# A row-sum kernel: its rows in three contiguous blocks of 16, 96 and 16 per partition, with all but the last 16 results stored early

## The chip, the cores and the metric

The kernel runs on one core of one Trainium2 chip. The metric is the device time of one execution in microseconds, the lower the better.

Two clocks appear in the text. The *time* is what a run is judged by. The *span* is what the profile covers: from the first to the last instruction of the program. A load or store has *landed* when the last of its 16 completions, one per DMA engine, has arrived at its semaphore (a counter on which engines wait).

## The reference

```python
batch, seq, dim = 32, 512, 1024
x = randn(batch, seq, dim).astype(float32)
out = sum(maximum(x, 0), axis=-1)     # float32, shape (32, 512)
```

There are 16384 rows of 1024 floats: 64 MiB are read, 64 KiB are written. Each of the 128 partitions handles 128 rows (J = 128), and `res` holds one result per row, so it is a 128 x 128 tile.

## The kernel before

All input and output DMAs are issued by SP (SyncE) on one queue; ACT is ScalarE, DVE is VectorE. Rows are loaded in seven chunks of 16 rows per partition (8 MB each), into three buffers, then in a tail of 8, 4, 2 and 1 rows, and the last row in two halves of 512 columns. For most chunks ACT applies the relu and DVE sums. In the last full chunk and in the tail both engines do whole rows alone, with an accumulating instruction each.

```python
x0 = xr[0 : P * BIG, :].rearrange("(p j) d -> p j d", p=P)     # block of 16 rows per partition
o0 = of[0 : P * BIG].rearrange("(p j) -> p j", p=P)
xv = xr[P * BIG :, :].rearrange("(p j) d -> p j d", p=P)       # block of 112 rows per partition
ov = of[P * BIG :].rearrange("(p j) -> p j", p=P)
# ... cut: chunks, then the tail loads, from xv ...
sp.dma_start(out=o0[:, :], in_=res[:, 0:BIG]).then_inc(s_out0, 16)    # behind the last load
# ... cut: the compute of chunks and tail ...
act.wait_ge(s_in[-2], 16)          # first half of the last row
on_act(buf[:, tb, BIG - 1, 0 : LAST[0]], last[:, LAST[1] : LAST[1] + 1]).then_inc(s_tact, 1)
dve.wait_ge(s_tact, 1)
dve.wait_ge(s_in[-1], 16)          # second half, with ACT's sum as its 513th column
on_dve(last[:, :], res[:, J - 1 : J]).then_inc(s_tdve, 1)
sp.wait_ge(s_tdve, 1)
sp.dma_start(out=ov[:, :], in_=res[:, BIG:J]).then_inc(s_out, 16)     # 112 results per partition
```

The partition pitch of a block is its number of rows times 4 KB: 64 KB in the block of 16, 448 KB in the block of 112. In the output a partition's results of a block lie in one row: 64 B for 16 rows, 448 B for 112.

Of the kernel before, what the change touches and what calls it, by code (L numbers as in the profile page):

```python
# [2 lines left out]

P = 128
D = 1024
BIG = 16
NBIG = 7
NTWO = 6
NB = 3
STEPS = [4, 5, 7]  # L10
MIXED = [3, 4, 5]
TAIL = [8, 4, 2, 1]
LAST = [512, 512]


def bass_relu_sum_kernel(
    nc: bass.Bass,
    x: bass.AP,
    out: bass.AP,
):  # L20






    fp32 = mybir.dt.float32
    ALU = mybir.AluOpType
    AF = mybir.ActivationFunctionType
    X = mybir.AxisListType.X  # L30

    B, S, _ = x.shape
    J = B * S // P
    assert BIG * NBIG + sum(TAIL) + 1 == J and sum(LAST) == D

    xr = x.rearrange("b s d -> (b s) d")
    of = out.rearrange("b s -> (b s)")
    x0 = xr[0 : P * BIG, :].rearrange("(p j) d -> p j d", p=P)
    o0 = of[0 : P * BIG].rearrange("(p j) -> p j", p=P)
    xv = xr[P * BIG :, :].rearrange("(p j) d -> p j d", p=P)  # L40
    ov = of[P * BIG :].rearrange("(p j) -> p j", p=P)

    buf = nc.alloc_sbuf_tensor("buf", [P, NB, BIG, D], fp32)
    last = nc.alloc_sbuf_tensor("last", [P, LAST[1] + 1], fp32)
    res = nc.alloc_sbuf_tensor("res", [P, J], fp32)

    n_in = NBIG + len(TAIL) + 2
    s_in = [nc.alloc_semaphore(f"s_in{i}") for i in range(n_in)]
    s_act = nc.alloc_semaphore("s_act")
    s_dve = nc.alloc_semaphore("s_dve")  # L50
    s_tact = nc.alloc_semaphore("s_tact")
    s_tdve = nc.alloc_semaphore("s_tdve")
    s_out0 = nc.alloc_semaphore("s_out0")
    s_out = nc.alloc_semaphore("s_out")

    sp, act, dve = nc.sync, nc.scalar, nc.vector


    tb = NBIG % NB
    for c in range(NBIG + 1):  # L60
        if c >= NB:
            sp.wait_ge(s_dve, 3 * (c - NB + 1))
        if c < NBIG:
            sp.dma_start(  # L64
                out=buf[:, c % NB, :, :],
                in_=xv[:, (c - 1) * BIG : c * BIG, :] if c else x0[:, :, :],
            ).then_inc(s_in[c], 16)
    r = 0
    tail = []
    for i, n in enumerate(TAIL):  # L70
        sp.dma_start(  # L71
            out=buf[:, tb, r : r + n, :],
            in_=xv[:, (NBIG - 1) * BIG + r : (NBIG - 1) * BIG + r + n, :],
        ).then_inc(s_in[NBIG + i], 16)
        tail.append((r, n, s_in[NBIG + i]))
        r += n
    sp.dma_start(
        out=buf[:, tb, r, 0 : LAST[0]], in_=xv[:, J - BIG - 1, 0 : LAST[0]]
    ).then_inc(s_in[-2], 16)
    sp.dma_start(out=last[:, 0 : LAST[1]], in_=xv[:, J - BIG - 1, LAST[0] : D]).then_inc(  # L80
        s_in[-1], 16
    )
    sp.dma_start(out=o0[:, :], in_=res[:, 0:BIG]).then_inc(s_out0, 16)


    def on_act(t, acc):
        return act.activation(t, t, AF.Relu, accum_out=acc)  # L87

    def on_dve(t, acc):
        return dve.tensor_scalar(  # L90
            out=t, in0=t, scalar1=0.0, scalar2=None, op0=ALU.max, op1=ALU.add, accum_out=acc
        )

    def row(c, i):
        return buf[:, c % NB, i, :], res[:, c * BIG + i : c * BIG + i + 1]

    for c in range(NTWO):
        b, steps = c % NB, STEPS if c < NTWO - 1 else MIXED
        act.wait_ge(s_in[c], 16)
        if steps is MIXED:  # L100
            dve.wait_ge(s_in[c], 16)
            for i in (BIG - 4, BIG - 3):
                on_dve(*row(c, i))
        r = 0
        for i, n in enumerate(steps):
            t = buf[:, b, r : r + n, :]
            act.activation(t, t, AF.Relu).then_inc(s_act, 1)  # L107
            dve.wait_ge(s_act, 3 * c + i + 1)
            dve.tensor_reduce(  # L109
                out=res[:, c * BIG + r : c * BIG + r + n], in_=t, axis=X, op=ALU.add  # L110
            ).then_inc(s_dve, 1)
            r += n
        if steps is MIXED:
            for i in (BIG - 2, BIG - 1):
                on_act(*row(c, i))


    j0 = NBIG * BIG
    for c in range(NTWO, NBIG):
        act.wait_ge(s_in[c], 16)  # L120
        dve.wait_ge(s_in[c], 16)
        for i in range(BIG):
            (on_act if i % 2 else on_dve)(*row(c, i))
    for r, n, s in tail:
        if n > 1:
            act.wait_ge(s, 16)
        dve.wait_ge(s, 16)
        for i in range(r, r + n):
            f = on_act if (i - r) % 2 else on_dve
            f(buf[:, tb, i, :], res[:, j0 + i : j0 + i + 1])  # L130

    act.wait_ge(s_in[-2], 16)
    on_act(buf[:, tb, BIG - 1, 0 : LAST[0]], last[:, LAST[1] : LAST[1] + 1]).then_inc(s_tact, 1)
    dve.wait_ge(s_tact, 1)
    dve.wait_ge(s_in[-1], 16)
    on_dve(last[:, :], res[:, J - 1 : J]).then_inc(s_tdve, 1)


    sp.wait_ge(s_tdve, 1)
    sp.dma_start(out=ov[:, :], in_=res[:, BIG:J]).then_inc(s_out, 16)  # L140
    sp.wait_ge(s_out0, 16)
    sp.wait_ge(s_out, 16)


# [1 line left out]
_INS = ['x']  # L146
_OUTS = [((32, 512), 'float32')]


# [21 lines left out]
```

## Time and profile before

| | before |
|---|---|
| time, median of the first 3 runs | 162.49 us (162.36 to 162.69) |
| span of the profile | 161.04 us |
| DMA queue, share of 16 engines | 97.1% |
| last piece of the last load completes | 158.57 us |
| last DVE piece | 158.72 to 159.41 us |
| final store, issue to last completion | 159.44 to 161.00 us |

First the page's DMA part of the kernel before (queue and kind, then packets, megabytes and the share of the 16 engines' span).

```profile
q1 hardware_dynamic: 2160, 67.18, 97.1%
HBM read 67.11 MB, written 0.07 MB: 417 GB/s over the span
```

The 16 DMA engines are busy nearly the whole span, so the loads set the time. The packet records of the trace show how evenly: a 64 KB row takes 2.418 us (median; 27.1 GB/s per engine), and the chunks after the first land 19.35 us apart. Now the end of the chain that ended last (start in us, duration, what):

```profile
123.74 34.20 DMA buf<-in_x_dram
157.94 0.02 issue
157.96 0.73 ACT buf L87 x2
158.70 0.02 issue
158.72 0.70 DVE last L90 x2
```

And the DMA issues of the stores (size of one, median us from issue to landing), with the timeline's line of the final one (start, duration on the queue):

```profile
out_dram<-res SPq DMA_DIRECT2D x1, 56.0 KB, 1.6
out_dram<-res SPq DMA_DIRECT2D x1, 8.0 KB, 34.0
```

```profile
159.44 0.34 SPq L140 DMA_DIRECT2D out_dram<-res  x1
```

The early 8 KB store stood 34 us in the queue behind loads, and nobody waited for it. The 56 KB store stands alone behind everything: ACT piece, DVE piece, store, end. Only what shortens this serial end, or the loads, shortens the span. Of the store's 1.56 us, 0.34 us is the issue on SP, about 0.5 us passes until the first packet at 160.28, the packets run until 160.62, and completions come until 161.00.

### The profile page before, as it was taken

The numbers are of one execution on the slowest core, as the hardware profiler recorded it, in microseconds if no ns is written. First come the engines' busy times: TensorE is split into PE (matmuls) and PEld (weight loads), VectorE is DVE, ScalarE is ACT, GpSimd is POOL, SyncE is SP. The second block draws the span as 40 slices with busy tenths as digits, with TensorE's granted clock in tenths as the row PEclk, the third lists the DMA queues.
The fourth block names the chain that finished last, engine by engine and source line by source line (L and its number), as shares of the span: only waits on it lengthen the run. The fifth ranks groups of instructions, "written<-read, shape, count | busy, mean of one in ns | idle before, by whom it ended". The sixth has DMA issues, their size and how long they took to land.

```text
span 161.0 us, 144 instructions
## 1 busy us (share of the span) xinstructions
DVE 122.0 (76%) x56; ACT 101.0 (63%) x55; POOL 0.2 (0%) x4
## 2 busy tenths in 40 slices
DVE  0000004998969898898969989699899999598995
ACT  3000039991599907997099951999339980596972
POOL 0000000000000000000000000000000000000000
DMA  7979979979979979979979979979979969999992
GB/s 260 521 309 472 521 309 472 521 309 472 521 309 472 521 309 472 521 309 472 521 309 472 521 309 472 521 309 472 521 309 472 521 260 521 391 391 431 413 403 71
DMA packets 2160, 67.18 MB, mean 417 GB/s; under 512 B 496, under 2 KB 496, under 8 KB 880
## 3 DMA queue, kind: packets, MB, share of 16 engines
q1 hardware_dynamic: 2160, 67.18, 97.1%
HBM read 67.11 MB, written 0.07 MB: 417 GB/s over the span
## 4 chain that ended last, share of the span: by engine, by line
DMA 69%; ACT 18%; DVE 10%; SPq 1%; issue 0%
DMA buf<-in_x_dram 69%; ACT buf L107 17%; DVE res L109 9%; SPq L71 1%; ACT buf L87 0%; DVE last L90 0%; SPq L64 0%
## 5 line engine op out<-in xcount | busy, mean ns | idle before, releaser
L109 DVE TENSOR_REDUCE res<-buf 128x4 f32<-128x4096 f32 (+3 forms) x18 | 100.4, 5604 | 34.5 <-ACT buf L107 34.5
L107 ACT ACTIVATE buf<-buf 128x4096 f32<-128x4096 f32 (+3 forms) x18 | 80.9, 4555 | 47.3 <-DMA buf<-in_x_dram 47.3
L87 ACT ACTIVATE buf<-buf 128x1024 f32<-128x1024 f32 (+1 forms) x18 | 18.4, 1024 | 9.7 <-DMA buf<-in_x_dram 9.7
L90 DVE TENSOR_SCALAR_CACHE_REDUCE buf<-buf 128x1024 f32<-128x1024 f32 x18 | 21.0, 1216 | 2.7 <-DMA buf<-in_x_dram 2.5
L87 ACT ACTIVATION_READ_ACCUMULATOR buf<-buf 128x1 f32 x18 | 3.4, 189 | 0.0
L107 ACT ACT_TABLE_LOAD x1 | 1.3, 1283 | 0.7 <-PEq L156 0.7
L90 DVE DVE_READ_ACCUMULATOR buf<-buf 128x1 f32 x18 | 1.5, 83 | 0.0
L90 DVE TENSOR_SCALAR_CACHE_REDUCE last<-last 128x513 f32<-128x513 f32 x1 | 0.7, 689 | 0.2 <-ACT buf L87 0.2
L156 POOL MEMSET const-bfloat16-1.0<- 128x1 bf16 x1 | 0.1, 102 | 0.0
L156 POOL MEMSET const-uint8-127<- 128x1 uint8 x1 | 0.1, 102 | 0.0
L156 POOL MEMSET const-float32-0.0<- 128x1 f32 x1 | 0.1, 99 | 0.2 <-issue 0.2
L156 POOL MEMSET const-float32-1.0<- 128x1 f32 x1 | 0.1, 99 | 0.0
L90 DVE DVE_READ_ACCUMULATOR last<-last 128x1 f32 x1 | 0.1, 84 | 0.0
## 6 DMA issues: line engine op xcount, KB each, us to landing
buf<-in_x_dram SPq DMA_DIRECT2D x1, 4096.0 KB, 26.7
buf<-in_x_dram SPq DMA_DIRECT2D x1, 2048.0 KB, 31.2
buf<-in_x_dram SPq DMA_DIRECT2D x1, 1024.0 KB, 33.2
buf<-in_x_dram SPq DMA_DIRECT2D x1, 512.0 KB, 34.0
buf<-in_x_dram SPq DMA_DIRECT2D x1, 256.0 KB, 34.2
last<-in_x_dram SPq DMA_DIRECT2D x1, 256.0 KB, 34.3
buf<-in_x_dram SPq DMA_DIRECT2D x7, 36.3
out_dram<-res SPq DMA_DIRECT2D x1, 56.0 KB, 1.6
```

The lines of the kernel that those rows point to most:

```text
L71: sp.dma_start(out=buf[:, tb, r : r + n, :], in_=xv[:, (NBIG - 1) * BIG + r : (NBIG - 1) * BIG + r + n, :],).then_inc(s_in[NBIG + i], 16)
L87: return act.activation(t, t, AF.Relu, accum_out=acc)
L90: return dve.tensor_scalar(out=t, in0=t, scalar1=0.0, scalar2=None, op0=ALU.max, op1=ALU.add, accum_out=acc)
L107: act.activation(t, t, AF.Relu).then_inc(s_act, 1)
L109: dve.tensor_reduce(out=res[:, c * BIG + r : c * BIG + r + n], in_=t, axis=X, op=ALU.add).then_inc(s_dve, 1)
L156: nc = _bacc.Bacc("TRN2", target_bir_lowering=False, num_devices=1)
```

## The change

The intent is to have nearly all results out before the end: the rows are cut into three blocks, the results of the first two are stored as soon as they are there, behind the last load in the queue, and the final store carries 16 results per partition (64 B rows, 8 KB) in place of 112.

```diff
-NBIG = 7
+REGIONS = [16, 96, 16]
+CHUNKS = [(0, 0), (1, 0), (1, 16), (1, 32), (1, 48), (1, 64), (1, 80)]
 ...
-    x0 = ...; o0 = ...; xv = ...; ov = ...            (as above, two blocks)
+    start = [sum(REGIONS[:i]) for i in range(len(REGIONS))]
+    xv = [xr[P * s : P * (s + n), :].rearrange("(p j) d -> p j d", p=P)
+          for s, n in zip(start, REGIONS)]
+    ov = [of[P * s : P * (s + n)].rearrange("(p j) -> p j", p=P) for s, n in zip(start, REGIONS)]
 ...   (chunks load from xv[g][:, j : j + BIG, :], the tail from xv[-1])
-    sp.dma_start(out=o0[:, :], in_=res[:, 0:BIG]).then_inc(s_out0, 16)
+    sp.wait_ge(s_fact, 1)
+    sp.wait_ge(s_fdve, 1)
+    for g in range(len(REGIONS) - 1):
+        sp.dma_start(out=ov[g][:, :], in_=res[:, start[g] : start[g] + REGIONS[g]]).then_inc(s_store, 16)
 ...   (last two rows of chunk 6:)
-            (on_act if i % 2 else on_dve)(*row(c, i))
+            ins = (on_act if i % 2 else on_dve)(*row(c, i))
+            if i >= BIG - 2:
+                ins.then_inc(s_fact if i % 2 else s_fdve, 1)
 ...
-    sp.dma_start(out=ov[:, :], in_=res[:, BIG:J]).then_inc(s_out, 16)
+    sp.dma_start(out=ov[-1][:, :], in_=res[:, start[-1] : J]).then_inc(s_out, 16)
```

Two things change at once: the size of the final store, and where each partition's rows lie (chunks 1 to 6 have a pitch of 384 KB in place of 448, the tail 64 KB in place of 448).

More of the change, by code (lines that the diff above doesn't have):

```diff
@@ L33, in bass_relu_sum_kernel @@
     J = B * S // P
-    assert BIG * NBIG + sum(TAIL) + 1 == J and sum(LAST) == D
+    NBIG = len(CHUNKS)
+    assert BIG * NBIG + sum(TAIL) + 1 == J == sum(REGIONS) and sum(LAST) == D
     xr = x.rearrange("b s d -> (b s) d")
     of = out.rearrange("b s -> (b s)")
-    x0 = xr[0 : P * BIG, :].rearrange("(p j) d -> p j d", p=P)
-    o0 = of[0 : P * BIG].rearrange("(p j) -> p j", p=P)
-    xv = xr[P * BIG :, :].rearrange("(p j) d -> p j d", p=P)
-    ov = of[P * BIG :].rearrange("(p j) -> p j", p=P)
+    start = [sum(REGIONS[:i]) for i in range(len(REGIONS))]
+    xv = [
+        xr[P * s : P * (s + n), :].rearrange("(p j) d -> p j d", p=P)
+        for s, n in zip(start, REGIONS)
+    ]
+    ov = [of[P * s : P * (s + n)].rearrange("(p j) -> p j", p=P) for s, n in zip(start, REGIONS)]
     buf = nc.alloc_sbuf_tensor("buf", [P, NB, BIG, D], fp32)
@@ L50, in bass_relu_sum_kernel @@
     s_dve = nc.alloc_semaphore("s_dve")
+    s_fact = nc.alloc_semaphore("s_fact")
+    s_fdve = nc.alloc_semaphore("s_fdve")
     s_tact = nc.alloc_semaphore("s_tact")
     s_tdve = nc.alloc_semaphore("s_tdve")
-    s_out0 = nc.alloc_semaphore("s_out0")
+    s_store = nc.alloc_semaphore("s_store")
     s_out = nc.alloc_semaphore("s_out")
@@ L63, in bass_relu_sum_kernel @@
         if c < NBIG:
-            sp.dma_start(
-                out=buf[:, c % NB, :, :],
-                in_=xv[:, (c - 1) * BIG : c * BIG, :] if c else x0[:, :, :],
-            ).then_inc(s_in[c], 16)
+            g, j = CHUNKS[c]
+            sp.dma_start(out=buf[:, c % NB, :, :], in_=xv[g][:, j : j + BIG, :]).then_inc(
+                s_in[c], 16
+            )
     r = 0
@@ L70, in bass_relu_sum_kernel @@
     for i, n in enumerate(TAIL):
-        sp.dma_start(
-            out=buf[:, tb, r : r + n, :],
-            in_=xv[:, (NBIG - 1) * BIG + r : (NBIG - 1) * BIG + r + n, :],
-        ).then_inc(s_in[NBIG + i], 16)
+        sp.dma_start(out=buf[:, tb, r : r + n, :], in_=xv[-1][:, r : r + n, :]).then_inc(
+            s_in[NBIG + i], 16
+        )
         tail.append((r, n, s_in[NBIG + i]))
         r += n
-    sp.dma_start(
-        out=buf[:, tb, r, 0 : LAST[0]], in_=xv[:, J - BIG - 1, 0 : LAST[0]]
-    ).then_inc(s_in[-2], 16)
-    sp.dma_start(out=last[:, 0 : LAST[1]], in_=xv[:, J - BIG - 1, LAST[0] : D]).then_inc(
+    sp.dma_start(out=buf[:, tb, r, 0 : LAST[0]], in_=xv[-1][:, BIG - 1, 0 : LAST[0]]).then_inc(
+        s_in[-2], 16
+    )
+    sp.dma_start(out=last[:, 0 : LAST[1]], in_=xv[-1][:, BIG - 1, LAST[0] : D]).then_inc(
         s_in[-1], 16
     )
-    sp.dma_start(out=o0[:, :], in_=res[:, 0:BIG]).then_inc(s_out0, 16)
+    sp.wait_ge(s_fact, 1)
+    sp.wait_ge(s_fdve, 1)
+    for g in range(len(REGIONS) - 1):
+        sp.dma_start(
+            out=ov[g][:, :], in_=res[:, start[g] : start[g] + REGIONS[g]]
+        ).then_inc(s_store, 16)
     def on_act(t, acc):
@@ L139, in bass_relu_sum_kernel @@
     sp.wait_ge(s_tdve, 1)
-    sp.dma_start(out=ov[:, :], in_=res[:, BIG:J]).then_inc(s_out, 16)
-    sp.wait_ge(s_out0, 16)
+    sp.dma_start(out=ov[-1][:, :], in_=res[:, start[-1] : J]).then_inc(s_out, 16)
+    sp.wait_ge(s_store, 16 * (len(REGIONS) - 1))
     sp.wait_ge(s_out, 16)
```

## The prediction

> **What bounds the kernel.** The loads, at the rate of the 16 DMA engines. The page gives the queue 97.1% of 16 engines' span, 417 GB/s on average. In the trace's packet records every 64 KB row of a full chunk takes 2.418 us (27.1 GB/s per engine) once the start is over, both in chunk 0 (neighbouring partitions 64 KB apart) and in chunks 1 to 6 (448 KB apart); chunks land 19.35 us apart. The chain of waits is 69% DMA, but its ACT and DVE parts lie beside running loads.
>
> After the last load comes a short serial end (chain, timeline): the 512-column ACT piece ends at 158.70 us, the last DVE piece runs 158.72 to 159.41, the final store (56 KB, 128 rows of 448 B) is issued at 159.44, its packets run 160.28 to 160.62, its last completion arrives at 161.00, the end of the span: 1.56 us from issue to landing.
>
> **What the change does.**
> - Bytes, chunks, compute and the order of loads stay. Rows move: chunks 1 to 6 get a partition pitch of 384 KB for 448 KB, the tail 64 KB. The Trainium skill, "DMA: Bandwidth & Descriptors", section Latency and other measured facts, shows losses at 2 MiB pitch and above, and a better rate at 512 KiB. This trace agrees as far as it goes: 64 and 448 KB both give 2.418 us. I expect 0 us.
> - The store of the first 16 columns and a new one of 96 (384 B rows, 48 KB) are issued once chunk 6 is done, about 148.1 us in the timeline; both should be issued by 149.2, after all loads. They drain behind the last load. Before, the 64 B store there took 0.06 us per engine and landed at 158.75, 0.18 us after the last load. With the 384 B rows (0.15 us per engine, scaled from the 448 B store's 0.177) they should land at 158.9 to 159.2, over 1 us before the final store's packets. Cost: 0.
> - The final store shrinks to 64 B rows. An engine's packets take 0.177 us for 8 rows of 448 B and 0.057 us for 8 of 64 B. Gain: about 0.12 us, wholly on the critical path. The rest, about 1.4 us of issue, start and completion, stays: the same section says that tiny transfers do not go below about 800 ns whatever their size, and here last packet to completion alone was 0.39 us. It may rise a little for 64 B rows (0.59 us in the early 64 B store, though behind loads), so I count 0.1 us.
> - Two more increments and waits: off the path.
>
> **Prediction.** 162.49 minus 0.1: 162.38 us; 8 in 10 between 162.05 and 162.68. Faster by over 2%: 0.01; within 2%: 0.96; slower by over 2%: 0.03. The spread of before (0.33 us) exceeds the gain, so the medians may not show its sign.
>
> **What would show it.** Right: chunks land 19.35 us apart; last load completes near 158.57, last DVE piece ends near 159.4; the two stores are issued near 148 to 149 and complete before 159.3; the final store takes about 1.45 us from issue to landing; span about 160.9.
> Wrong: row packets above 2.42 us in chunks 1 to 6 (pitch matters); final store still 1.56 us or more (a fixed latency hides the bytes); the last load's completion later, or the final store's packets starting over 0.9 us after its issue (the extra stores are in its way).
>
> **What would break it.** A memory conflict at 384 KB pitch: 5% on six of eight chunks would add about 6 us. Or the stores behind the last load delaying its completion or the final store, some tenths of a us.

## The result, and the profile after

The changed kernel took 162.44 us (median of 6 runs, 162.30 to 162.69), the kernel before 162.53 us (6 runs, 162.33 to 162.71). The ratio is 0.9996, with a 95% interval of 0.9983 to 1.0009. A ratio is the mean time of one kernel's fast runs over that of the other's of the same rounds, so it is not quite the ratio of the medians.

The same lines of the kernel after: queue, end of the chain, stores, and the stores in the timeline.

```profile
q1 hardware_dynamic: 2304, 67.18, 97.5%
HBM read 67.11 MB, written 0.07 MB: 418 GB/s over the span
```

```profile
157.89 0.73 ACT buf L98 x2
158.62 0.03 issue
158.65 0.69 DVE last L101 x2
```

```profile
out_dram<-res SPq DMA_DIRECT2D x1, 48.0 KB, 10.3
out_dram<-res SPq DMA_DIRECT2D x2, 8.0 KB, 5.9
```

```profile
148.14 0.82 SPq L92 DMA_DIRECT2D out_dram<-res  x2
159.37 0.33 SPq L153 DMA_DIRECT2D out_dram<-res  x1
```

The reader should see three things. The two early stores are issued at 148.14 us, as soon as chunk 6 is done, and they land 10.3 us later because loads stand ahead of them. The chain up to the final store has the same parts, with the same durations within 0.02 us. (The "5.9" is the median of the two 8 KB stores, one of about 10.4 and one of 1.40 us.) The final store runs from 159.37 to its last completion at 160.77, which is 1.40 us.

Packet records tell where those 0.15 us came from. From the final store's first packet until the first engine was through with its eight rows it took 0.177 us at 448 B and 0.054 us at 64 B; that is 0.12 us. The rest is a few hundredths in the issue, the start and the completion.

The two profiles differ by 0.22 us in span (161.04 and 160.82), but one profile of each is a poor witness: how soon the first chunk lands varies by 0.2 us between executions of one kernel, as the first experiment shows. So the experiments below are compared by *stages* of the trace, and by the times and spans of five rounds.

### The profile page after: what moved, and what is told of

Same layout as the page of the kernel before. It is cut to its first block, busy times and chain, and to the rows that moved or that the text cites. A ratio compares the mean times of both kernels' runs of the same rounds, so it can differ in the third digit from the quotient of the medians.

```text
span 160.8 us, 146 instructions
## 1 busy us (share of the span) xinstructions
DVE 122.0 (76%) x56; ACT 101.0 (63%) x55; POOL 0.2 (0%) x4
## 4 chain that ended last, share of the span: by engine, by line
DMA 69%; ACT 18%; DVE 10%; SPq 1%; issue 0%
DMA buf<-in_x_dram 69%; ACT buf L118 17%; DVE res L120 9%; SPq L78 1%; ACT buf L98 0%; DVE last L101 0%; SPq L72 0%
## 6 DMA issues: line engine op xcount, KB each, us to landing
out_dram<-res SPq DMA_DIRECT2D x1, 48.0 KB, 10.3
```

## The experiments

Twelve runs were made, in four groups; three of them repeat a kernel (before_again, after_again, split_again). A group shares a chip and its executions of the kernel before. Each run had five rounds, and each was correct. These are stages read from the trace of every kernel (semaphore landings and packet records, us; "last load" is the last completion of the last load):

| kernel | chunk 0 landed | chunk 1 to 5 landed after it | chunk 5 to last load | last load to end | final store, issue to landing |
|---|---|---|---|---|---|
| before | 22.75 | 96.76 | 39.06 | 2.42 | 1.55 |
| before_again | 22.52 | 96.73 | 39.04 | 2.44 | 1.56 |
| after | 22.69 | 96.74 | 39.10 | 2.24 | 1.40 |
| after_again | 22.57 | 96.75 | 39.07 | 2.24 | 1.39 |
| split_only | 22.53 | 96.74 | 39.07 | 2.25 | 1.41 |
| split_again | 22.49 | 96.75 | 39.04 | 2.26 | 1.41 |
| one_block | 23.18 | 96.95 | 38.98 | 2.51 | 1.54 |
| final_4B | 22.68 | 96.72 | 39.11 | 7.86 | 7.02 |
| four_apart | 22.63 | 96.74 | 39.06 | 2.25 | 1.41 |
| stores_late | 22.70 | 96.75 | 39.14 | 3.32 | 1.49 |
| stores_ahead | 22.60 | 96.75 | 39.17 | 2.28 | 1.41 |
| three_pieces | 22.55 | 96.72 | 39.42 | 2.02 | 1.41 |
| split_three | 22.65 | 96.74 | 39.13 | 2.09 | 1.41 |
| dve_pad | 22.70 | 96.75 | 39.05 | 2.27 | 1.41 |

("Chunk 1 to 5 landed after it" is the time from chunk 0's last completion to that of the sixth load, chunk 5; the stage after it holds chunk 6, the tail and the last row.) The semaphore lists are unrounded, so 1.55 here is the 1.56 that the rounded times of the chain give.

And the times. (The record gives a span to 0.1 us, so each "time minus span" is good to 0.05 us.)

| kernel | median us | ratio to before (95%) | mean span us | time minus span, us |
|---|---|---|---|---|
| before_again | 162.41 | 1.0000 (0.9988 to 1.0012) | 160.84 | 1.59 to 1.68 |
| split_only | 162.22 | 0.9982 (0.9970 to 0.9994) | 160.64 | 1.32 to 1.62 |
| one_block | 163.12 | 1.0040 (1.0027 to 1.0053) | 161.55 | 1.40 to 1.71 |
| final_4B | 168.71 | 1.0379 (1.0366 to 1.0392) | 166.30 | 2.17 to 2.47 |
| stores_late | 163.40 | 1.0055 (1.0042 to 1.0069) | 161.80 | 1.55 to 1.71 |
| stores_ahead | 162.44 | 0.9997 (0.9984 to 1.0009) | 160.92 | 1.52 to 1.63 |
| three_pieces | 162.10 | 0.9979 (0.9966 to 0.9991) | 160.80 | 1.32 to 1.40 |
| after_again | 162.35 | 1.0001 (0.9988 to 1.0013) | 160.80 | 1.45 to 1.69 |
| split_again | 162.33 | 0.9994 (0.9980 to 1.0007) | 160.64 | 1.46 to 1.73 |
| four_apart | 162.37 | 1.0000 (0.9988 to 1.0013) | 160.72 | 1.62 to 1.72 |
| split_three | 162.01 | 0.9977 (0.9965 to 0.9990) | 160.68 | 1.31 to 1.40 |
| dve_pad | 162.25 | 0.9990 (0.9977 to 1.0004) | 160.86 | 1.34 to 1.37 |

### before_again: the noise

No edit.

> The kernel before, unchanged, against itself: sets the noise of the times and gives a second profile. Both theories: ratio 1.000. Theory (row bytes of the final store): its issue to landing is again 1.56 us within 0.04, its packets of one engine again about 0.18 us. Rival (the 1.56 against 1.40 us of the two first profiles is scatter between profiles): this profile may show anything from 1.40 to 1.60.

The ratio is 1.0000, and the interval of plus or minus 0.0012 (0.2 us) is the resolution of everything below. The final store took 1.56 us again, so that figure is no scatter. But the span was 0.28 us shorter than in the first profile of the same kernel, 0.23 of it because chunk 0 landed earlier. The rival falls for the store; scatter lives at the start.

### split_only and split_again: the stores without the new layout

```diff
 (kernel before, two blocks of 16 and 112; waits on chunk 6 added as in the change)
     sp.dma_start(out=o0[:, :], in_=res[:, 0:BIG]).then_inc(s_out0, 16)
+    sp.dma_start(out=ov[:, 0:96], in_=res[:, BIG:112]).then_inc(s_out0, 16)
 ...
-    sp.dma_start(out=ov[:, :], in_=res[:, BIG:J]).then_inc(s_out, 16)
+    sp.dma_start(out=ov[:, 96:112], in_=res[:, 112:J]).then_inc(s_out, 16)
```

> The layout of before (two blocks, 16 and 112 rows per partition); the first 96 columns of the second block are stored early, behind the last load, and the final store is 16 columns: 128 rows of 64 B that lie 448 B apart in the output, not in one contiguous piece. Theory (only the bytes of a row count): final store 1.40 us from issue to landing as in after, within 0.04. Rival (the contiguous 8 KB target of the third block is what helps): stays at 1.5 to 1.56 us. Loads 2.418 us per 64 KB row in both.

The stores of split_only, as the DMA issues list them:

```profile
out_dram<-res SPq DMA_DIRECT2D x1, 48.0 KB, 10.4
out_dram<-res SPq DMA_DIRECT2D x2, 8.0 KB, 5.9
```

They read as those of after, and the final store took 1.41 us: it needs no contiguous target. The third block is not what helps. Its ratio, 0.9982, was lower than that of after, so both ran again side by side:

> The changed kernel again, next to split_again on the same chip. Theory (the final store's rows are worth 0.12 to 0.16 us, and the 384 KB pitch gives some of it back, 0 to 0.15 us): ratio to before 0.9990 to 1.0000; 64 KB rows after the first 8 us longer on average than the 2.420 us of the layout of before. Rival (no difference of layout, the low times of split_only were chance): ratio equal to that of split_again within 0.0005.

> The early stores and the 64 B final rows on the layout of before, again. Theory: ratio to before 0.9980 to 0.9992, below after_again; 64 KB rows 2.420 us on average after the first 8 us; final store 1.40 us. Rival: as after_again.

The pair gave 1.0001 and 0.9994, with intervals that overlap. By the times alone the difference is not shown. By the spans, which leave out the scatter outside them, it is more visible: after_again had 160.80 us (160.7, 160.9, 160.8, 160.7, 160.9), split_again 160.64 (160.6, 160.6, 160.6, 160.7, 160.7), and before, in the same group, 160.86 (nine runs). The other runs agree: 160.92 for after (six runs), and 160.80 to 160.92 for the three later kernels on the new layout that have early stores behind or ahead of the last load (three_pieces, dve_pad, stores_ahead), but 160.64 for split_only and 160.72 and 160.68 for four_apart and split_three on the old one. So in spans the early stores are worth about 0.2 us on the old layout and 0 to 0.1 on the new one, although the final store is equally short in both. Both forecasts of the pair were missed by a little: after_again came out at 1.0001 where 0.9990 to 1.0000 was expected, and its 64 KB rows were not longer on average (2.420 us); split_again came out at 0.9994 where 0.9980 to 0.9992 was expected.

That the new layout loses the difference, some 0.15 us, in the loads is not shown. Chunk 0 has the same addresses in both layouts, and its landing scatters by 0.2 us. From its landing to that of the last load, the five profiles on the old layout with the same load pieces took 135.77 to 135.82 us, and the five on the new one without stores ahead (after, after_again, final_4B, whose last block is split once more, stores_late and dve_pad) 135.80 to 135.89: a loss of 0 to 0.1 us. To the end of the final store it was 138.05 to 138.06 us in split_only, split_again and four_apart, and 138.07 to 138.09 in after, after_again and dve_pad.

Single rows do show the layout in some profiles. In the five profiles that have the load layout and the load pieces of the kernel before (before, before_again, both splits and four_apart), 13 to 15 of the 64 KB rows after the first 8 us took more than 2.45 us, and the 4 KB rows of the tail took 0.161 to 0.162 us on average and 0.25 us at most. On the new layout it was 57 rows of 64 KB in after, 54 in final_4B and 89 in stores_late, but 17 in after_again and 14 in dve_pad; the 4 KB rows took 0.170 and 0.171 us on average in after and after_again, up to 0.33 and 0.37 us. Little of this reaches the last completion, as the stages show.

### one_block: one block of 128 rows, one store at the end

```diff
-REGIONS = [16, 96, 16]
-CHUNKS = [(0, 0), (1, 0), ..., (1, 80)]
+REGIONS = [128]
+CHUNKS = [(0, 0), (0, 16), (0, 32), (0, 48), (0, 64), (0, 80), (0, 96)]
 (tail from row 112 of the block; no early store, so the final store is 64 KB in 512 B rows)
```

> One block of 128 rows per partition (pitch 512 KB), no early store at all, one final store of 64 KB with 512 B rows. Theory: pitch does not matter (64 KB rows stay at 2.42 us, chunks 19.35 us apart), and the final store takes 1.40 us plus 448 B more per row on 8 rows of an engine, about 0.13 to 0.16 us: 1.53 to 1.60 us; total about 162.5. Rival 1 (pitch matters): row packets above 2.45 us and a total over 164. Rival 2 (early stores behind the last load cost something): the last load lands earlier after its packets than the about 0.4 us of before and after.

The beginning of its chain, and then that of after:

```profile
1.15 41.35 DMA buf<-in_x_dram
42.50 0.02 issue
```

```profile
1.16 40.86 DMA buf<-in_x_dram
42.02 0.02 issue
```

The final store took 1.54 us, inside the expected 1.53 to 1.60. The total did not come as expected: 163.12 us, a ratio of 1.0040. The loads are late from the start. Chunk 0 landed at 23.18 us in place of 22.5 to 22.75, and chunks 1 to 5 lost another 0.2 us. The median row still took 2.418 us, but eight rows that start near 41 us took 2.7 to 2.98. Between the first and the last of the 16 engines' completions lay 1.06 us at chunk 0 and 1.15 us at chunk 5, where the two profiles of the kernel before showed 0.77 and 0.45 at chunk 5. A chunk has landed when its slowest engine is done, and the lag of chunk 0 is still there at chunk 5. The theory "pitch does not matter" falls; the figure of rival 1 (over 164 us) was too large. That the loss comes from the pitch is likely, as this is the only thing that changed for the loads; how the pitch delays an engine is not shown. Rival 2 finds no support: the last load's completion came 0.44 us after its last packet, against 0.47 in before and 0.40 in after.

### final_4B and four_apart: rows of 4 B

final_4B goes on in the direction of the change, with a block of one row per partition at the end:

```diff
-REGIONS = [16, 96, 16]
+REGIONS = [16, 96, 15, 1]
 ...
+    sp.wait_ge(s_r2act, 1); sp.wait_ge(s_r2dve, 1)          # the 15 columns are done
+    sp.dma_start(out=ov[2][:, :], in_=res[:, start[2] : start[3]]).then_inc(s_store, 16)
     sp.wait_ge(s_tdve, 1)
     sp.dma_start(out=ov[-1][:, :], in_=res[:, start[-1] : J]).then_inc(s_out, 16)
```

> Four blocks (16, 96, 15, 1): the final store has 4 B rows, 512 B in all, still 128 packets; the 15 columns before it are stored about 0.6 us ahead of it. Theory (bytes at the engines' rate plus a few ns per packet, on a fixed rest of 1.34 us): no more than 0.02 to 0.03 us below after, 1.37 to 1.40 us. Rival (writes under some size cost more, or several engines writing one small piece of memory disturb each other): 1.45 us or more.

Its two last stores (15 columns, then the last one):

```profile
out_dram<-res SPq DMA_DIRECT2D x1, 7.5 KB, 2.3
out_dram<-res SPq DMA_DIRECT2D x1, 0.5 KB, 7.0
```

The smallest store of all took 7.0 us and made the kernel 3.8% slower. Its packets went out as quickly as ever (the last packet of after ended at 160.41 us, of this kernel at 160.38); the completions trickled in from 162.58 to 166.37. The 15-column store before it, 60 B rows one behind the other, took 2.3 us. The theory is wrong, and the rival was right; it named two causes, and four_apart tells them apart. It stores the same 15 columns and then the same single column, but into the two-block layout, where neighbouring partitions' pieces lie 448 B apart:

```diff
 (split_only)
-    sp.dma_start(out=ov[:, 96:112], in_=res[:, 112:J]).then_inc(s_out, 16)
+    sp.dma_start(out=ov[:, 96:111], in_=res[:, 112:127]).then_inc(s_out0, 16)   (as soon as they are done)
+    sp.dma_start(out=ov[:, 111:112], in_=res[:, 127:J]).then_inc(s_out, 16)     (after s_tdve)
```

> As split_only, but the final store is one column, 4 B rows that lie 448 B apart in the output; the 15 columns before it go 0.9 us earlier. Theory A (the 7.0 us of the contiguous 4 B rows came from many small writes into the same small piece of memory): here about 1.4 us from issue to landing, total as split_only. Theory B (a write below some size is slow wherever it lands): about 7 us, total about 168. In between: both.

```profile
out_dram<-res SPq DMA_DIRECT2D x1, 7.5 KB, 1.4
out_dram<-res SPq DMA_DIRECT2D x1, 0.5 KB, 1.4
```

With the same number of packets and the same bytes both stores take 1.4 us. So a small write is not slow in itself; here the small writes that lay one behind the other were. Rows of 64 B, one behind the other (after, 1.40 us), are free of it, rows of 60 B are not (2.3 us), and rows of 4 B least of all. That would fit pieces of memory of 64 B that several writes share, but this cause is not shown: only these three sizes were tried. And 4 B rows gain nothing over 64 B rows: 1.41 us.

### stores_late: is the early place worth anything?

```diff
-    (behind the last load)   wait for chunk 6; store blocks 0 and 1
+    (after s_tdve)           store blocks 0 and 1, then the final store
```

> After, but the stores of 16 and 96 columns are issued only once the last DVE piece is done, right before the final store. Theory (the early place hides them wholly; an issue takes SP 0.34 to 0.45 us): the final store is issued about 0.8 us later, and ends about 0.8 us later: total about 0.8 us above after. Rival (the queue takes all three together): under 0.3 us.

```profile
159.55 0.82 SPq L150 DMA_DIRECT2D out_dram<-res  x2
160.42 0.43 SPq L153 DMA_DIRECT2D out_dram<-res  x1
```

The final store is issued 0.87 us after the first of the three and takes 1.49 us. The mean span is 161.80, against 160.80 and 160.92 of after. So the cost is 0.9 to 1.0 us, close to the theory's 0.8, and 0.87 of it is the later issue of the final store. Hiding the stores matters; the kernel before needs no hiding, as it has only one store at the end.

### stores_ahead: is the place behind the last load needed?

```diff
+    sp.dma_start(out=ov[0][:, :], in_=res[:, 0:16]).then_inc(s_store, 16)      (ahead of the tail loads)
+    sp.dma_start(out=ov[1][:, 0:64], in_=res[:, 16:80]).then_inc(s_store, 16)
 ...
-    (behind the last load)   store blocks 0 and 1
+    sp.dma_start(out=ov[1][:, 64:96], in_=res[:, 80:112]).then_inc(s_store, 16)
```

> After, but 16 + 64 columns are stored ahead of the tail loads in the queue and only 32 columns behind the last load. Theory (what stands ahead of the last load costs the engines its packet time, what stands behind costs nothing): the last load lands 0.15 to 0.25 us later (64 B and 256 B rows, 16 packets per engine), the end too. Rival (the place in the queue is of no matter): last load lands as in after, 158.5 within 0.08 from the span's start.

This stayed undecided. The last load landed at 158.52 us, as the rival had it, but that number contains the scatter of the start. The step that the stores stand in, from chunk 6 to the first piece of the tail, took 9.82 us, against 9.70 and 9.72 in after and after_again: about 0.11 us, less than the theory's 0.15 to 0.25. The ratio, 0.9997, is that of after. In this profile the stores ahead of the loads cost about a tenth of a microsecond.

### three_pieces and split_three: a shorter last piece

Both cut the last row in three, one on the new layout and one on the old:

```diff
-LAST = [512, 512]
+LAST = [512, 256, 256]
 ...
 (ACT: the first 512, as before)
+    dve.wait_ge(s_in[-2], 16)
+    on_dve(buf[:, tb, BIG - 1, 512:768], last[:, 257:258]).then_inc(s_mdve, 1)
+    dve.wait_ge(s_mdve, 1)
     dve.wait_ge(s_tact, 1)
     dve.wait_ge(s_in[-1], 16)
     on_dve(last[:, :], res[:, J - 1 : J]).then_inc(s_tdve, 1)        (258 columns in place of 513)
```

> After, with the last row in pieces of 512, 256 and 256 columns in place of 512 and 512; ACT takes the first, DVE the second, and DVE the third together with the two sums. The serial end after the last load is then a 258 column piece in place of 513. Theory (the end is a chain: last load, last DVE piece, final store): last DVE piece ends about 0.2 us earlier, total 0.15 to 0.25 us below after, the lowest of all kernels. Rival (an extra load piece and an extra DVE wait eat it): within 0.05 us of after.

> split_only with the last row in pieces of 512, 256 and 256 columns, as three_pieces has them. Theory (both gains lie on the chain after the last load and add up): from the last load's landing to the end 2.02 us as in three_pieces, against 2.25 in split_only; total 0.1 to 0.25 us below split_again, the lowest of all. Rival (the extra load piece costs what the shorter last piece gains): equal to split_again within 0.1 us.

The last DVE piece of split_three, and its final store, in the timeline:

```profile
158.75 0.42 DVE L98 TENSOR_SCALAR_CACHE_REDUCE last<-last 128x258 f32<-128x258 f32 x1
159.09 0.08 DVE L98 DVE_READ_ACCUMULATOR last<-last 128x1 f32 x1
```

```profile
159.21 0.33 SPq L153 DMA_DIRECT2D out_dram<-res  x1
```

Both came out lowest in time, at 162.10 and 162.01 us, and split_three is the fastest of the study: 0.9977 of the kernel before, an interval that leaves out 1. The totals fell in the direction of the forecasts and by a little more (medians 0.25 and 0.34 us below after_again and after, where 0.15 to 0.25 was expected; 0.32 us below split_again, where 0.1 to 0.25 was). The reason is not the forecast one. The chain after the last load did shrink, from 2.26 to 2.09 us in split_three (2.02 was expected), but the extra load piece delayed the last load (39.13 in place of 39.04 us; in three_pieces 39.42 in place of 39.10 and 39.07), and the mean span did not shrink at all: 160.68 us against 160.64 of split_again. The last DVE piece itself became 0.27 us shorter (0.69 to 0.42 us), but it started 0.23 us after the last load had landed, where split_again waited 0.13: DVE was still at the piece before it until 158.71 us. The whole gain of split_three over split_again, 0.3 us in the medians, lies *outside* the span: time minus span fell to 1.31 to 1.40 us in all ten runs of the two kernels, against 1.46 to 1.73 in split_again. No expectation had that.

### dve_pad: what shortens the time outside the span?

The packet records hold one 8 KB packet of the kind "instruction" near the end of each profile. It starts at 160.79 and 160.47 us in three_pieces and split_three, within 0.15 us of the final store's last completion, and about 1.4 us after the final store's last completion in the others (162.20 us in after), except for the first profile of the kernel before, which records none. Compared with after, the trace of three_pieces has two more DVE instructions, the added piece and its accumulator read (and one more load). The first line of the page, busy time and instructions, for after and then for three_pieces:

```profile
DVE 122.0 (76%) x56; ACT 101.0 (63%) x55; POOL 0.2 (0%) x4
```

```profile
DVE 122.0 (76%) x58; ACT 101.0 (63%) x55; POOL 0.2 (0%) x4
```

So the last run was the kernel after with two useless DVE instructions:

```diff
+    pad = nc.alloc_sbuf_tensor("pad", [P, 2], fp32)
+    dve.memset(pad[:, 0:1], 0.0)
+    dve.memset(pad[:, 1:2], 0.0)
```

> After, with two memsets of one unused column each at the start of DVE's program, where DVE idles for 26 us. They do no work that the kernel needs. It asks where three_pieces and split_three got the half of their gain that their spans do not show: time minus span was 1.31 to 1.40 us in their ten runs, and mostly 1.5 to 1.7 in every other kernel but final_4B. Theory (the two extra DVE instructions moved a fetch of instructions, an 8 KB packet of kind instruction, from after the end of the span into the time of the last store): span as in after, 160.7 to 161.0, but time minus span 1.3 to 1.4 us, total about 162.15, the packet before 161. Rival (the shorter remainder comes from the shorter last piece or the extra load, not from DVE's instruction count): time minus span 1.5 to 1.7, total 162.35 to 162.45, the packet near 162.1.

Its queue lines show the packet inside the span now (the second line, 0.01 MB):

```profile
q1 hardware_dynamic: 2304, 67.18, 97.4%
q14 instruction: 1, 0.01, 0.0%
```

The packet starts at 160.65 us, time minus span is 1.34 to 1.37 us in all five runs, and the span is that of after, 160.86 us. The time is 162.25 us, the ratio 0.9990. So the theory held for the remainder and for the place of the packet; the total lies between the two forecasts, and its interval (0.9977 to 1.0004) includes no change. Two instructions that compute nothing took 0.15 to 0.24 us, on average, from the time outside the span: 1.35 us here, against 1.51 in the kernel before of the same group and 1.59 in after_again. The smaller figure is the safer one, as it compares executions on one chip; the kernel before showed 1.32 to 1.69 us in its nine runs there, so the remainder is not fixed without the two instructions either. That the earlier fetch is what shortens the remainder is inferred from three kernels in which the two go together; which engine fetches, and what the end of the program waits for, is not shown.

## Why the prediction was right

- *The loads set the time, and the change leaves them.* Right in the main: chunks 1 to 6 land 19.33 to 19.39 us apart in both kernels. The step "I expect 0 us" for the pitch was nearly right: by the prediction's own test the median row stayed at 2.418 us, but 57 of 848 rows took over 2.45 us in after (15 in before), and the loads after chunk 0 lost 0 to 0.1 us. The spans of five executions differ by 0.16 us (after_again 160.80, split_again 160.64), which these stages do not account for. At 512 KB the whole kernel lost 0.65 us against the kernel before, whose final store is no shorter (1.56 us against 1.54). The prediction leaned here on the Trainium skill, "DMA: Bandwidth & Descriptors", section Latency and other measured facts, which gives a better rate at 512 KiB than at 2 MiB and above; one_block shows a small loss already at 512 KB.
- *The early stores cost nothing behind the last load.* Right as far as the runs show: issued at 148.14 us, the last load landed at 158.53 (forecast near 158.57), and the stores completed by 158.85 us (forecast before 159.3). stores_late shows what they cost in the open, 0.9 to 1.0 us.
- *The final store loses about 0.12 us of packet time, of which 0.1 us was counted.* Right in kind, a little small: packets lost 0.12 us, the whole store 0.15. The fear that small rows complete later did not come true for 64 B: from the last packet's end to the last completion it was 0.37 us, against 0.38.
- *The rest, about 1.4 us, stays.* Right: no final store took less than 1.39 us, and all those of 64 B rows that were issued alone took 1.39 to 1.41, as did the 4 B rows that lay apart. The Trainium skill, "Perfetto Trace Analysis", section DMA Instruction — HWDGE, says that a DMA's completion waits for the write to be confirmed and that this "can cause a surprisingly long delay especially when the write target is HBM"; the traces show such a delay, 0.34 to 0.38 us after the last packet in the final stores of 64 B rows and more, and 5.99 us in final_4B, but not its cause.
- *The total.* 162.38 forecast, 162.44 measured, inside the range, and within 2% as expected. The gain of 0.09 us in the medians is smaller than the noise, as the prediction said. So the total is no test of the mechanism: the kernel before, at 162.53, lies in the range too, and that 162.44 fell so near the forecast is partly luck. The stages are the test. From the landing of chunk 0 to the end the two profiles of the kernel before took 138.25 and 138.20 us, and after and after_again 138.09 and 138.07: a gain of 0.12 to 0.18 us, with 0.18 to 0.19 won after the last load and 0 to 0.07 lost in the loads.

So the change was nearly neutral because it could only cut some 0.15 us, the bytes of the last store, from 162.5 us, and the start (by 0.2 us) and the time outside the span (by 0.2 to 0.4 us) scatter by more. Whether its layout cost some of the gain in the executions that were not profiled stays open. The kernel before with the same early stores and no third block is at least as good, and split_three has the lowest time.

## What to carry to other kernels

In this kernel, which is bound by its loads, a change of the stores could shorten only the serial end after the last load, and the final store had a floor (1.4 us) that its bytes hardly touched. For a kernel like it: hide all other stores behind the loads, keep the remaining rows large enough (64 B here) or far enough apart (448 B here) that their completions do not drag, and leave the input's layout alone unless that is needed. Test a change that does two things by doing each alone; here the part that looked essential (a contiguous target) was not needed. Where a few tenths matter, compare the stages of the traces and the spans as well as the times, because a gain can be right in size and come from somewhere else.

## What the Trainium skill lacked or had wrong

- "DMA: Bandwidth & Descriptors": it does not say that neighbouring small rows disturb one another. 128 rows of 4 B took 7.02 us one behind the other and 1.41 us at 448 B apart; rows of 60 B took 2.3 us and 1.4 us.
- "DMA: Bandwidth & Descriptors", section Specifications: it calls 512 B the minimum for line rate, with a read-modify-write below. For an isolated final store no step showed at 512 B: 1.54 us for 512 B rows, 1.56 for 448 B, 1.40 for 64 B. These are times of a whole small store, so they do not contradict a figure that is about rate.
- "DMA: Bandwidth & Descriptors", section Latency and other measured facts: its row pitch figures stop at 512 KiB as the good case. Here loads with a 512 KB pitch landed chunk 0 0.4 to 0.7 us later than with 64 KB, and with 384 KB in place of 448 KB the loads after chunk 0 took 0 to 0.1 us longer.
- "Runtime: NRT & Kernel Launch", section Instruction fetch mechanics: it speaks of 16 KiB blocks and a cost that is mostly hidden. Here the fetch near the end was an 8 KB packet, and with two instructions more on DVE the time outside the span was 1.34 to 1.37 us, where the kernel before of the same group had 1.32 to 1.69 (1.51 on average).
